# Encoder layer with attention, retention and a mixture of experts: retention moved beside the input projection, a block at a time, and the overflow tables moved two jobs later

## The chip, the cores and the metric

The program runs on one core of one Trainium2 chip. The metric is the device time of one execution, in microseconds (us), lower being better. TensorE (PE) does the matmuls, VectorE (DVE), ScalarE (ACT) and GpSimd (POOL) the elementwise work, and SyncE (SP) issues most of the transfers between HBM and the on-chip memories SBUF and PSUM. Each engine runs its own queue of instructions strictly in order.

## The reference, cut to what matters

```python
xn = rmsnorm(x, attn_norm_g); proj = xn @ w_in          # 2048 x 1024 by 1024 x 3072
q_da, k_da, v_da, q_r, k_r, v_r, g_r = split(proj)
o_da = diff_attention(...)        # 4 heads, two softmax maps each, ALiBi, block-causal
# retention, 4 heads, chunkwise recurrent:
s = einsum(q, k * 64**-0.5) * decay ** (i - j)          # lower triangle
intra = s @ v
state = state * decay ** CHUNK + (k * k_decay).T @ v
o_r = silu(g) * head_rmsnorm(intra + (q * q_decay) @ state)
h = x + concat(o_da, o_r) @ w_out
xn = rmsnorm(h, ffn_norm_g)
out = rmsnorm(h + moe(xn), final_norm_g)                # 32 experts, 2 of them for each token
```

Only retention is changed in its formula: if a key is divided by its decay when it is written, then scores need no more than a mask, and what is left over is one factor for each query row, which a norm over the head removes, apart from its epsilon.

## The kernel before

All sizes are float32; large matmuls are made of three float32r products of a high and a low part (`mm3`: hi by hi, hi by lo, lo by hi), so each operand is first split by ACT (the high part, a copy) and DVE (the low part, a subtraction). The time falls into these parts.

- **The input projection** (`Proj.run`) goes through a list of units. A unit is one 128x512 piece of the projected columns for one group of 512 tokens or one block of 128 rows: 24 matmuls into the PSUM tile `pa`. Kind 2 is the values of attention, 1 and 0 its keys and queries, 3 the queries and keys of retention, 4 and 5 its values and gates. The list has three stages (token groups 0 and 1, then 2, then 3). In each stage of the kernel before, all kinds 2, 1 and 0 come first and 3, 4 and 5 last. The weights of a unit are loaded as `wr` and split into `whi` and `wlo`. Results go to scratch in HBM (`VS`, `KS`, `QS`, `RT`, `VR`, `GR`).
- **Attention** (`att_head`) runs for each stage and head over blocks of 128 queries: score matmuls into `pS`, each followed on DVE by one instruction that adds the distance bias and takes the maximum (`p<-pS,dist`, L352), the exponential on ACT, on DVE the difference of the two maps (`p<-p,c,p`, L366), then transposes into `pT`, a split of them on ACT and DVE (`ah` and `al`), and matmuls with the values into `pO`.
- **Retention** (`retention`) takes two blocks of 128 tokens at a time: POOL multiplies values and queries by decays (`vd`, `qd`) and finishes the outputs (`O`).
- **The output projection** (`OutProj`) loads and splits `w_out` (`woh`, `wol`), and then makes each block of 128 rows of `h` by matmuls into `pF`, its norm and its router logits.
- **The experts** (`experts`) run as 32 jobs. A job gathers its rows (`xg`), transposes them on DVE (`xT`), splits weights (`mh`, `ml`) and multiplies. Between the jobs' matmuls stand steps of `units` and `completion`, which make the tables for experts that overflow and the order in which rows are finished (tiles `u_...` and `c_...`); the first such step stands in job `SIDE`.

`merge` writes two parts into one program by their planned weights: attention beside the projection until a share `FA` of attention is written, then beside retention (`FR`), and the rest beside the output projection. `OutProj.steps` takes block b only when `k.ready` is over b, and block 11 only when all attention is written. A scheduler then fixes each engine's order.

Of the kernel before, what the change touches and what calls it, by code (L numbers as in the profile page):

```python
# [24 lines left out]
EPS = 1e-6  # L25
# [59 lines left out]
class Proj:  # L85


    def __init__(self, k, ctx):
# [15 lines left out]
        self.ready = set()  # L104
        self.nload = self.nsplit = 0
        units = []
        for s, gs in enumerate(STAGES):
            bs = [4 * g + i for g in gs for i in range(4)]
            units += [(2, b) for b in bs]
# [84 lines left out]
    def colT(self, u, c, ct, g):  # L194
# [8 lines left out]
        if c == 3:  # L203
            st = self.stg.tile([128, 512], F32, name="st", tag="st")
            nc.scalar.activation(st, ps, AF.Copy)
            nc.sync.dma_start(k.RT[ct][:, ts], st)
            return
# [9 lines left out]
    def rows(self, u, c, b):  # L217
# [14 lines left out]
        else:  # L232
            st = self.stg.tile([128, 512], F32, name="st", tag="st")
            nc.scalar.activation(st, ps, AF.Copy)
            nc.sync.dma_start((k.VR if c == 4 else k.GR)[bs, :], st)

    def run(self):
# [10 lines left out]
        for u, x in enumerate(self.units):  # L248
# [3 lines left out]
            elif n0 - 4 <= u < n0:  # L252
                nb = u - n0 + 12
            elif n0 + 4 <= u < n0 + 12 and u % 2 == 0:
                nb = (u - n0 - 4) // 2 + 12
# [9 lines left out]
            else:  # L265
                yield from self.rows(u, *x)


def attention(k, pj):

    with ExitStack() as ctx:
        att_psum(k, ctx)
        for s in range(len(STAGES)):
# [4 lines left out]
            with ExitStack() as c1:  # L278
                att_pools(k, c1, s)
                for h in range(4):  # L280
                    while (s, h) not in pj.ready:
                        yield 0
                    yield from att_head(k, s, h)
    k.att_done, k.ready = True, NB
    yield 0.1

# [9 lines left out]
def att_head(k, s, h):  # L296
# [26 lines left out]
    U = k.bu.tile([128, nq, 128], F32, name="U")  # L323
# [3 lines left out]
    def scores(i):  # L327

        if i % 2 == 0:
            q = k.bq.tile([128, 2, 2, 256], F32R, name="qs")  # L330
            for m in range(2):
                for d in range(2):
                    nc.sync.dma_start(q[d * 64:(d + 1) * 64, m].bitcast(F32),
                                      k.QS[h][:, m * 64:(m + 1) * 64, i * 128:(i + 2) * 128].rearrange("i d t -> d i t"))
            qs[0] = q
        o = i % 2 * 128
# [5 lines left out]
        for m in range(2):  # L342
# [4 lines left out]
            for n, (a0, a1) in enumerate(ch):  # L347
                acc = k.pS.tile([128, 512], F32, name="pS")
                x = acc[:, :a1 - a0]
                nc.tensor.matmul(x, qs[0][:, m, 0, o:o + 128], ks[m][:, a0:a1], start=True, stop=False)  # L350
                nc.tensor.matmul(x, qs[0][:, m, 1, o:o + 128], ks[m][:, a0:a1], start=False, stop=True)  # L351
# [17 lines left out]
    def values(j):  # L369
# [34 lines left out]
        oT = k.bo.tile([128, 256], F32, name="oT")  # L404
# [5 lines left out]
        jj = 2 * (j - 2 * g0)  # L410
        for ii in range(2):
            nc.scalar.activation(U[:, jj + ii], pt[:, 0, ii * 128:(ii + 1) * 128], AF.Square, accum_out=ss[:, jj + ii:jj + ii + 1])
        nc.scalar.activation(U[:, jj:jj + 2].rearrange("p a b -> p (a b)"), pt[:, 0], AF.Copy)
        yield 0.2

    def finish(b0, b1):
# [8 lines left out]
        u = U[:, b0:b1]  # L425
        nc.gpsimd.tensor_mul(u, u, r[:, :, None].to_broadcast([128, n, 128]))  # L426
        nc.gpsimd.tensor_mul(u, u, k.subg[:, None, :].to_broadcast([128, n, 128]))
# [8 lines left out]
    step = 2 if (s, h) == (len(STAGES) - 1, 3) else nq  # L436
    done = 0
    for j in range(n0, n1):
        yield from scores(2 * j)
        if j > n0:  # L440
            load_rest()
            yield from values(j - 1)
            if 2 * (j - n0) % step == 0:
                finish(done, done + step)
                done += step
                if step == 2:
# [6 lines left out]
def retention(k):  # L453
    nc, tc = k.nc, k.tc
    V, G = nc.vector, nc.gpsimd
    state, qz = [], {}
    for pr in range(2):
        s_ = k.br.tile([128, 128], F32, name=f"state{pr}", bufs=1)
        V.memset(s_, 0.0)
        state.append(s_)  # L460
        for n in range(2):
            z = k.br.tile([128, 2, 256], F32, name=f"qz{pr}{n}", bufs=1)
            V.memset(z[0:64, 1], 0.0)
            V.memset(z[64:128, 0], 0.0)
            qz[pr, n] = z
    def prepare(n):
        X = K()
        X.rows = ts = slice(n * 256, n * 256 + 256)
        X.kt = k.br.tile([128, 2, 256], F32, name="kt")
        for i in range(2):  # L470
            nc.sync.dma_start(X.kt[:, i], k.RT[2 + i][:, ts])
        X.q = [qz[pr, n % 2] for pr in range(2)]
        for pr in range(2):
            for s in range(2):
                nc.sync.dma_start(X.q[pr][s * 64:(s + 1) * 64, s], k.RT[pr][s * 64:(s + 1) * 64, ts])
        X.vr = k.br.tile([128, 2, 512], F32, name="vr")
        gr = k.br.tile([128, 2, 512], F32, name="gr")
        nc.sync.dma_start(X.vr, k.VR[ts, :].rearrange("(b p) n -> p b n", p=128))
        nc.sync.dma_start(gr, k.GR[ts, :].rearrange("(b p) n -> p b n", p=128))
        X.vd = k.br.tile([128, 2, 4, 128], F32, name="vd")  # L480
        G.tensor_mul(X.vd, X.vr.rearrange("p b (h e) -> p b h e", h=4),
                     k.vdec[:, None, :, None].to_broadcast([128, 2, 4, 128]))
        X.qd = []
        for pr in range(2):
            qd = k.br.tile([128, 2, 2, 128], F32, name=f"qd{pr}")
            G.tensor_mul(qd, X.q[pr].rearrange("p s (b t) -> p s b t", b=2),
# [1440 lines left out]
```

## Time and profile before

| | us |
|---|---|
| median of 3 runs | 2099.15 |
| lowest and highest of them | 2093.79, 2099.17 |
| the profiled execution's own time | 2083.01 |
| its span, first to last instruction | 2081.2 |

The rows below come from the profiled execution, and all times in them are counted from the start of its span. Its own time is 1.8 us more than the span, and 16.1 us under the median of the runs.

### The profile page before, as it was taken

How to read it: one execution, taken by the hardware profiler on the slowest of the kernel's cores; microseconds unless marked ns; L12 is line 12 of the kernel's file. 1: busy time of each engine (PE TensorE's matmuls, PEld its weight loads, DVE VectorE, ACT ScalarE, POOL GpSimd, SP SyncE). 2: the span in 40 equal slices, each digit the busy share in tenths (PEclk: the TensorE clock that was granted, in tenths of full speed). 3: DMA queues.
4: the chain of work that ended last, by engine and by line, in shares of the span. 5: the costliest groups of instructions: out<-in, count | busy, mean ns of one | idle time of the engine just before them, and what ended most of it. 6: DMA issues, size and time to landing. Idle time of an engine off the chain costs nothing.

```text
span 2081.2 us, 30110 instructions
## 1 busy us (share of the span) xinstructions
PE 1944.9 (93%) x9811; PEld 1543.9 (74%) x9811; DVE 1553.2 (75%) x3462; ACT 1122.7 (54%) x1915; POOL 673.7 (32%) x362
## 2 busy tenths in 40 slices
PE   7999999999999987789999996799999999999994
PEld 5788888878888875578887775577777677777673
DVE  7345446855565578987877767999988899998884
ACT  4244445634444454555454314676776787776663
POOL 0000000010000037421111105566867667875433
PEclk9999999999999998899999997799999999999997
DMA  6655344573675456463453455799999999998994
GB/s 201 193 153 171 117 135 144 178 242 129 195 213 167 137 160 215 128 203 132 156 183 111 138 223 182 254 304 296 338 343 320 319 339 349 353 344 302 338 316 117
DMA packets 241810, 459.61 MB, mean 221 GB/s; under 512 B 27376, under 2 KB 130160, under 8 KB 240624
## 3 DMA queue, kind: packets, MB, share of 16 engines
q1 hardware_dynamic: 224384, 401.53, 56.9%
q0 software_dynamic: 16976, 55.06, 9.8%
q8 instruction: 78, 1.28, 0.3%
q10 hardware_dynamic: 288, 1.05, 0.1%
q14 instruction: 84, 0.69, 0.1%
HBM read 365.81 MB, written 91.75 MB: 220 GB/s over the span
## 4 chain that ended last, share of the span: by engine, by line
PE 72%; DVE 9%; DMA 7%; issue 5%; SPq 2%; POOL 2%; ACT 2%; ACTq 0%; DVEq 0%; POOLq 0%
PE pa L63 7%; PE pa L62 7%; PE pa L64 7%; PE acc L63 7%; PE acc L62 7%; PE acc L64 7%; PE acc L72 4%; PE acc L74 3%; PE pS L350 3%; PE pS L351 3%; PE pT L382 2%; PE pF L62 2%; PE pF L64 2%; PE pF L63 2%; DMA wr<-in_w_in_dram 2%
## 5 line engine op out<-in xcount | busy, mean ns | idle before, releaser
L1485 DVE TENSOR_TENSOR ml<-mr,mh 128x1024 fp32r<-128x1024 f32 x376 | 446.5, 1214 | 38.6 <-ACT mh L1484 32.4
L1484 ACT ACTIVATE mh<-mr 128x1024 fp32r<-128x1024 f32 x376 | 385.5, 1055 | 124.0 <-PE acc L74 66.3
L1515 POOL DMA_INDIRECT xg<-XN,TA x120 | 270.0, 2250 | 64.3 <-issue 30.5
L352 DVE CUSTOM_DVE_ANT_0 p<-pS,dist 128x512 f32<-128x512 f32 (+1 forms) x320 | 188.0, 605 | 126.3 <-PE pS L351 118.5
L426 POOL TENSOR_TENSOR U<-U,r 128x512 f32<-128x512 f32 (+2 forms) x13 | 16.5, 1270 | 725.9 <-DVE r L40 623.9
L359 ACT ACTIVATE p<-p,nm 128x128 f32<-128x128 f32 (+15 forms) x128 | 153.9, 1203 | 111.8 <-DVE nm L358 111.5
L63 PE MATMUL acc<-ml,xhi 128*128 128x512 f32 x512 | 205.9, 403 | 5.0 <-DVE ml L1485 5.0
L64 PE MATMUL acc<-mh,xlo 128*128 128x512 f32 x512 | 206.2, 403 | 1.3 <-DVE xlo L1557 1.3
L62 PE MATMUL acc<-mh,xhi 128*128 128x512 f32 x512 | 204.0, 401 | 0.0
L54 ACT ACTIVATE ah<-pT 128x512 fp32r<-128x512 f32 (+2 forms) x176 | 85.4, 498 | 141.1 <-PE pT L382 99.6
L62 PE MATMUL pa<-xh,whi 128*128 128x512 f32 x384 | 152.9, 398 | 2.0 <-DVE nlam L633 2.0
L62 PE MATMUL pa<-whi,xh 128*128 128x512 f32 x384 | 151.8, 398 | 2.9 <-ACT whi L161 2.1
L63 PE MATMUL pa<-wlo,xh 128*128 128x512 f32 x384 | 153.1, 399 | 1.5 <-DVE nm L358 1.2
L64 PE MATMUL pa<-whi,xl 128*128 128x512 f32 x384 | 153.9, 401 | 0.0
L63 PE MATMUL pa<-xl,whi 128*128 128x512 f32 x384 | 151.8, 395 | 0.0
L64 PE MATMUL pa<-xh,wlo 128*128 128x512 f32 x384 | 151.6, 395 | 0.0
L350 PE MATMUL pS<-kst,qs 128*128 128x512 f32 (+1 forms) x320 | 123.5, 398 | 21.6 <-DVE cm L352 8.9
L162 DVE TENSOR_TENSOR wlo<-wr,whi 128x1024 fp32r<-128x1024 f32 x72 | 89.9, 1250 | 67.0 <-ACT whi L161 64.4
L55 DVE TENSOR_TENSOR al<-pT,ah 128x512 fp32r<-128x512 f32 (+2 forms) x176 | 97.5, 564 | 44.9 <-ACT ah L54 44.4
L62 PEld LDWEIGHTS acc<-mh,xhi 128*128 128x128 f32 x512 | 97.3, 190 | 31.8 <-ACT xhi L54 0.2
L161 ACT ACTIVATE whi<-wr 128x1024 fp32r<-128x1024 f32 x72 | 76.1, 1059 | 81.2 <-DMA wr<-in_w_in_dram 39.9
L63 PEld LDWEIGHTS acc<-ml,xhi 128*128 128x128 f32 x512 | 97.6, 191 | 28.9 <-DVE ml L1485 5.4
(536 smaller groups left out, 4912.5 us busy)
## 6 DMA issues: line engine op xcount, KB each, us to landing
mr<-in_expert_w_gate_dram SPq DMA_DIRECT2D x128, 512.0 KB
mr<-in_expert_w_up_dram SPq DMA_DIRECT2D x128, 512.0 KB
mr<-in_expert_w_down_dram SPq DMA_DIRECT2D x128, 512.0 KB
wr<-in_w_in_dram SPq DMA_DIRECT2D x72, 512.0 KB
vst<-VS SPq DMA_DIRECT2D x72, 256.0 KB
qs<-QS SPq DMA_DIRECT2D x128, 128.0 KB
st<-in_x_dram SPq DMA_DIRECT2D x16, 512.0 KB
VS<-st SPq DMA_DIRECT2D x32, 256.0 KB
```

What stands on the lines that cost most here:

```text
L54: nc.scalar.activation(hi, ps, AF.Copy)
L55: return nc.vector.tensor_sub(lo, ps, hi.bitcast(F32))
L62: nc.tensor.matmul(out, s_hi, m_hi, start=start, stop=False)
L63: nc.tensor.matmul(out, s_hi, m_lo, start=False, stop=False)
L64: nc.tensor.matmul(out, s_lo, m_hi, start=False, stop=stop)
L162: nc.vector.tensor_sub(lo, r, hi.bitcast(F32))
L350: nc.tensor.matmul(x, qs[0][:, m, 0, o:o + 128], ks[m][:, a0:a1], start=True, stop=False)
L352: nc.vector.tensor_tensor_reduce(p[:, a0:a1], x, tab[:, c0 + a0:c0 + a1], SLOPES[h], -3.0e38, OP.add, OP.max, accum_out=cm[:, n:n + 1])
L359: nc.scalar.activation(p[:, :nk], p[:, :nk], AF.Exp, bias=nm, accum_out=s0 if m == 0 else s1)
L1484: self.hi_at = nc.scalar.activation(hi, r, AF.Copy)
L1485: self.lo_at = nc.vector.tensor_sub(lo, r, hi.bitcast(F32))
L1515: nc.gpsimd.indirect_dma_start(out=xg[:, g * 256:(g + 1) * 256], out_offset=None, in_=v, in_offset=bass.IndirectOffsetOnAxis(ap=ix[:, g], ...
```

## The change

- Projection: in stages 0 and 2, kinds 3, 5 and 4 (in this order) follow the first head instead of the last. Keys of retention are multiplied by the inverse decay `kdec` as they leave PSUM (on DVE), and gates are written as silu(g) times two (tanh on ACT, one DVE instruction).
- `mixer` takes the place of `attention`: in stages 0 and 2 it writes retention (blocks 0 to 7, then 8 to 15) in turns with the attention of that stage, by `strands`, in proportion to planned weights. Stage 1 has attention alone. `mixers` goes on with `mixer` alone, after the projection, until the last block of retention is written (`k.kept_all`), and then merges what is left with the output projection.
- `retention` takes one block at a time; it uses the PSUM tiles `pT` of attention and `pt` of the projection. POOL's multiplications (`vd`, `qd`, `O`, `U`, half of `wol`) are gone: their work is left out by the new formula or done on DVE.
- The factor `subg` of attention's outputs goes into `w_out`. Queries of attention are loaded a block at a time with two buffers instead of two blocks at a time with one.
- Experts: `SIDE` is 3 instead of 1, and the rows of job 2 are transposed one step later (q 3 instead of q 2 of job 1).

```diff
 class Proj:
+            heads = []
             for h in range(4):
-                units += [(1, h, g) for g in gs] + [(0, h, g, s) if g == gs[-1] else (0, h, g) for g in gs]
-            units += [(3, h, g) for h in range(4) for g in gs]
-            units += [(c, b) for c in (4, 5) for b in bs]
+                heads.append([(1, h, g) for g in gs] + [(0, h, g, s) if g == gs[-1] else (0, h, g) for g in gs])
+            rest = [(3, h, g) for h in range(4) for g in gs] + [(c, b) for c in (5, 4) for b in bs]
+            if s != 1:
+                heads.insert(1, rest)
+            else:
+                heads.append(rest)
+            units += [(2, b) for b in bs] + sum(heads, [])
...
+                a = heads()
+                if s != 1:
+                    b0, b1 = RB[s]
+                    with k.tc.tile_pool(name=f"br{s}", bufs=2, reuse_waits="tile") as k.br:
+                        yield from until(lambda: k.kept == b1, (a, att_weight(s)), (retention(k, pj, b0, b1), (b1 - b0) * R_W))
+                    k.kept_all = b1 == NB
+                yield from a
+            if s < 2:
+                k.ready = 512 * (STAGES[s][-1] + 1) // 128
...
+RB = {0: (0, 8), 2: (8, 16)}
+R_W = 3.8
...
-        nc.gpsimd.tensor_mul(u, u, r[:, :, None].to_broadcast([128, n, 128]))
-        nc.gpsimd.tensor_mul(u, u, k.subg[:, None, :].to_broadcast([128, n, 128]))
+        u = U[0] if end else U[0][:, b0:b1]
+        nc.vector.tensor_mul(u, u, r[:, :, None].to_broadcast([128, n, 128]))
...
+            po = pj.pst.tile([128, 4, 128], F32, name="pt").rearrange("p a b -> p (a b)")
             for s in range(2):
+                h = 2 * pr + s
+                v = X[pr][1][:, s * 128:(s + 1) * 128]
                 if b:
+                    nc.tensor.matmul(po[:, s * 128:(s + 1) * 128], qz[pr][:, s], k.state[pr], start=True, stop=False)
+                nc.tensor.matmul(po[:, s * 128:(s + 1) * 128], A[:, s], v, start=not b, stop=True)
+                if b < NB - 1:
+                    nc.tensor.matmul(po[s * 64:(s + 1) * 64, 256:384], kd[:, s], v, start=True, stop=True)
...
+        for h in range(4):
+            V.scalar_tensor_tensor(th[:, h], O[:, h], r[:, h:h + 1], th[:, h], op0=OP.mult, op1=OP.mult)
...
 def mixers(k, outer):
-    na = att_weight()
+    na = sum(att_weight(s) for s in range(3))
+    nr = NB * R_W
...
-        merge(tc, pj.run(), 96 * 5.1 + 16 * 1.9, a, na * FA, 76)
+        merge(tc, pj.run(), 96 * 5.1 + 16 * 1.9, a, na * FA + nr, 76)
+        while not k.kept_all:
+            with tc.high_priority(PRI):
+                next(a)
     router_setup(k)
-        ret_consts(k)
-        merge(tc, retention(k), 58, a, na * FR)
...
-        merge(tc, op.blocks(at), OB, a, na * (1 - FA - FR))
+        merge(tc, op.blocks(at), OB, a, na * (1 - FA))
...
-SIDE = 1
+SIDE = 3
...
-                if q == 2 and n + 1 < 32:
-                    if n < 31:
-                        loads(n - 2)
-                    if n:
+                if q == 2 and n < 31:
+                    loads(n - 2)
+                if q == (3 if n == 1 else 2) and n + 1 < 32:
+                    if n == 1:
+                        with tc.issue_after(m.lo_at.ins):
+                            m.rows(jobs[2])
+                    elif n:
                         m.rows(jobs[n + 1])
```

How the queues stand, at three places. The first is PE at the end of the input projection in the kernel before: the last matmuls of the projection (`pa`), then attention, among which the first of retention (`pF<-qz,kt`) follows some 30 rows on.

```order
L62 MATMUL pa<-whi,xh_4227 128x512
L63 MATMUL pa<-wlo,xh_4227 128x512
L64 MATMUL pa<-whi,xl_4228 128x512
L62 MATMUL pO<-ah,vst 128x256
L350 MATMUL pS<-kst,qs 128x512
L351 MATMUL pS<-kst,qs 128x512
L350 MATMUL pS<-kst,qs 128x512
L351 MATMUL pS<-kst,qs 128x512
L63 MATMUL pO<-al,vst 128x256
```

In the changed kernel the same place reads as follows, and 1,208 PE instructions of attention and of retention's blocks 8 to 15 stand between the last `pa` and the first matmul of the output projection, where 594 (346 of attention, 248 of retention) stood before.

```order
L64 MATMUL pa<-xh_4949,wlo 128x512
L62 MATMUL pa<-xh_4949,whi 128x512
L63 MATMUL pa<-xl_4950,whi 128x512
L64 MATMUL pa<-xh_4949,wlo 128x512
L417 MATMUL pS<-kst,qs 128x512
L418 MATMUL pS<-kst,qs 128x512
L417 MATMUL pS<-kst,qs 128x512
L418 MATMUL pS<-kst,qs 128x512
L476 MATMUL pT<-ident,oT 128x128 x2
L449 MATMUL pT<-ident,p_5733 128x128
```

The second place is PE at the first matmuls of the output projection (`pF<-woh,mh`) in the changed kernel, which stand among the score matmuls of the last head.

```order
L417 MATMUL pS<-kst,qs 128x512
L418 MATMUL pS<-kst,qs 128x512
L792 MATMUL pF<-ident,mx 128x128 x8
L417 MATMUL pS<-kst,qs 128x384
L418 MATMUL pS<-kst,qs 128x384
L62 MATMUL pF<-woh,mh 128x512
L63 MATMUL pF<-wol,mh 128x512
```

Behind it 166 PE instructions of attention are left, where 614 were left before. The third place is PE in job 1 of the experts, before: the tables' matmul `pt<-u_tri,u_w` stands ahead of the transposes `pt<-ident,sg` of job 0's hidden rows.

```order
L62 MATMUL acc<-mh,xhi 128x512
L63 MATMUL acc<-ml,xhi 128x512
L64 MATMUL acc<-mh,xlo 128x512
L1282 MATMUL pt<-u_tri,u_w 128x32
L1594 MATMUL pt<-ident,sg 128x128 x4
L1287 MATMUL pt<-ident,u_w 128x32
L62 MATMUL acc<-mh,hhi 128x512
```

In the changed kernel those transposes stand earlier, among the matmuls of job 1, and the tables' matmul comes 193 rows later.

```order
L62 MATMUL acc<-mh,xhi 128x512
L63 MATMUL acc<-ml,xhi 128x512
L64 MATMUL acc<-mh,xlo 128x512
L62 MATMUL acc<-mh,xhi 128x512
L1651 MATMUL pt<-ident,sg 128x128 x4
L62 MATMUL acc<-mh,xhi 128x512
L63 MATMUL acc<-ml,xhi 128x512
```

## Rows read from the trace of the kernel before

**Rows 1.** Page, part 1: busy time of each engine, its share, instructions.

```profile
PE 1944.9 (93%) x9811; PEld 1543.9 (74%) x9811; DVE 1553.2 (75%) x3462; ACT 1122.7 (54%) x1915; POOL 673.7 (32%) x362
```

**Rows 2.** Tiles `wlo`, `wol`, `woh`, `pa`: min/median/max ns, first and last start in us.

```profile
L162 DVE TENSOR_TENSOR wlo<-wr,whi x72: 1215/1224/3108, 10.7 to 709.5; 128x1024 fp32r<-128x1024 f32 x72
...
L64 PE MATMUL pa<-whi,xl x384: 387/393/775, 14.7 to 736.8; 128*128 128x512 f32 x192
...
L713 DVE TENSOR_TENSOR wol<-wor,woh x4: 1207/1390/2111, 902.4 to 908.9; 128x1024 fp32r<-128x1024 f32 x4
...
L62 PE MATMUL pF<-woh,mh x256: 387/393/632, 912.1 to 1247.2; 128*128 128x512 f32 x128
```

**Rows 3.** Busy time by stage: length, PE, PEld, DVE, ACT, POOL, clock, DMA.

```profile
0.00:709.50 709.50, 686.75 (x3443) 574.42 (x3444) 408.34 (x1147) 317.25 (x632) 27.74 (x55) 1.00 0.55 170
709.50:737.20 27.70, 27.70 (x145) 23.41 (x144) 14.16 (x46) 11.17 (x21) 2.33 (x2) 1.00 0.39 114
737.20:902.40 165.20, 125.87 (x789) 100.59 (x788) 140.36 (x364) 86.91 (x286) 88.05 (x49) 0.88 0.54 175
912.10:1248.10 336.00, 326.10 (x2027) 269.93 (x2025) 253.82 (x866) 139.25 (x263) 41.25 (x34) 0.99 0.48 161
1248.10:1325.00 76.90, 46.58 (x181) 35.52 (x182) 61.16 (x158) 35.44 (x43) 50.35 (x28) 0.69 0.55 188
```

**Rows 4.** PE in order of time, 693.9 to 694.5 us: start, duration, instruction.

```profile
693.95 0.40 PE L351 MATMUL pS<-kst,qs 128*128 128x512 f32 x1
694.19 0.28 PE L63 MATMUL pO<-al,vst 128*128 128x256 f32 x1
694.31 0.28 PE L64 MATMUL pO<-ah,vst 128*128 128x256 f32 x1
```

**Rows 5.** Groups on DVE, shapes apart: busy us, mean ns | idle before them.

```profile
L352 DVE CUSTOM_DVE_ANT_0 p<-pS,dist 128x512 f32<-128x512 f32 x224 | 150.8, 685 | 78.9 <-PE pS L351 71.3 <-PE pT L382 6.1
L55 DVE TENSOR_TENSOR al<-pT,ah 128x512 fp32r<-128x512 f32 x112 | 75.3, 685 | 39.8 <-ACT ah L54 39.5
...
L502 DVE TENSOR_TENSOR A<-pF,rdec 128x256 f32<-128x256 f32 x32 | 13.3, 415 | 3.2 <-PE pF L500 3.1
L491 DVE SCALAR_TENSOR_TENSOR th<-th,gr 128x1024 f32<-128x1024 f32 x8 | 11.4, 1430 | 2.3 <-DMA qs<-QS 2.3
L530 DVE SCALAR_TENSOR_TENSOR state<-state,sdec,pF 128x128 f32<-128x128 f32 x30 | 10.2, 339 | 7.1 <-PE pF L528 6.8
L352 DVE CUSTOM_DVE_ANT_0 p<-pS,dist 128x128 f32<-128x128 f32 x32 | 9.2, 287 | 24.5 <-PE pS L351 24.5
L40 DVE SCALAR_TENSOR_TENSOR r<-t,r 128x4 f32<-128x4 f32 x21 | 3.3, 159 | 0.5
```

**Rows 6.** The same, 790 to 900 us: two groups.

```profile
L352 DVE CUSTOM_DVE_ANT_0 p<-pS,dist 128x512 f32<-128x512 f32 x32 | 21.5, 680 | 2.6 <-PE pS L351 2.6
...
L366 DVE SCALAR_TENSOR_TENSOR p<-p,c,p 128x1664 f32<-128x1664 f32 x2 | 6.8, 3418 | 0.0
```

**Rows 7.** The same, 930 to 1160 us: two groups.

```profile
L366 DVE SCALAR_TENSOR_TENSOR p<-p,c,p 128x2048 f32<-128x2048 f32 x3 | 7.0, 2346 | 0.1
...
L366 DVE SCALAR_TENSOR_TENSOR p<-p,c,p 128x1664 f32<-128x1664 f32 x2 | 3.9, 1952 | 0.1
```

**Rows 8.** Busy time in three shorter stretches, columns as in the stages.

```profile
770.00:800.00 30.00, 22.76 (x139) 18.14 (x138) 19.42 (x57) 11.46 (x56) 20.98 (x12) 0.82 0.90 284
810.00:900.00 90.00, 65.39 (x417) 52.09 (x416) 84.70 (x210) 51.53 (x144) 41.42 (x20) 0.91 0.41 138
1170.00:1247.00 77.00, 73.66 (x410) 56.79 (x407) 59.35 (x309) 16.54 (x39) 3.79 (x4) 0.98 0.56 213
```

**Rows 9.** PE's waits, 1248 to 1325 us: waited for, us, times, longest.

```profile
PE pt L1282 <- DVE u_w L1291: 10.8, 1, 10.8
PE acc L63 <- DVE ml L1485: 5.0, 1, 5.0
```

**Rows 10.** DVE's waits, 1281 to 1325 us.

```profile
DVE xT L1554 <- DMA xg<-XN,TA: 7.1, 1, 7.1
```

More of the change, by code (lines that the diff above doesn't have):

```diff
@@ L266, in run, with strands, mixer @@
                 yield from self.rows(u, *x)
-def attention(k, pj):
+                if x[0] == 4:
+                    self.rt = x[1] + 1
+def strands(*gs):
+    st = [[g, w, w, 0.0, False] for g, w in gs]
+    while st:
+        for x in sorted(st, key=lambda x: x[3] / x[2]):
+            w = next(x[0], None)
+            if w is None:
+                st.remove(x)
+                break
+            if w == 0:
+                x[4] = True
+                continue
+            if x[4]:
+                x[4] = False
+                for y in st:
+                    y[2], y[3] = max(y[1], 0.1), 0.0
+            x[1] -= w
+            x[3] += w
+            yield w
+            break
+        else:
+            yield 0
+def mixer(k, pj):
     with ExitStack() as ctx:
         att_psum(k, ctx)
+        ret_consts(k, ctx)
         for s in range(len(STAGES)):
@@ L279, in attention, with heads, until @@
                 att_pools(k, c1, s)
[L280 to L283, printed above, removed]
+                def heads():
+                    for h in range(4):
+                        while (s, h) not in pj.ready:
+                            yield 0
+                        yield from att_head(k, s, h)
+                a = heads()
[7 more added lines that the diff above has]
+                k.ready = 512 * (STAGES[s][-1] + 1) // 128
     k.att_done, k.ready = True, NB
     yield 0.1
+def until(done, *gs):
+    for w in strands(*gs):
+        yield w
+        if done():
+            return
+RB = {0: (0, 8), 2: (8, 16)}
+R_W = 3.8
 S_W = 0.108
@@ L327, in scores @@
     def scores(i):
[L329 to L336, printed above, removed]
+        for ii in (i, i + 1):
+            if ii not in qs and ii < 4 * g1:
+                q = qs[ii] = k.bq.tile([128, 2, 2, 128], F32R, name="qs")
+                for m in range(2):
+                    for d in range(2):
+                        nc.sync.dma_start(q[d * 64:(d + 1) * 64, m].bitcast(F32),
+                                          k.QS[h][:, m * 64:(m + 1) * 64, ii * 128:(ii + 1) * 128].rearrange("i d t -> d i t"))
+        q = qs.pop(i)
         nk = (i + 1) * 128
@@ L435, in load_rest @@
             pass
-    step = 2 if (s, h) == (len(STAGES) - 1, 3) else nq
+    step = 2 if end else nq
     done = 0
@@ L445, in att_head @@
                 done += step
-                if step == 2:
+                if end and h == 3:
                     k.ready = 4 * g0 + done
@@ new lines, in inner @@
+    def inner(kt, pr):
+        pa = k.pT.tile([128, 2, 256], F32, name="pT").rearrange("p a b -> p (a b)")
+        nc.tensor.matmul(pa[:, :256], kt, qz[pr], start=True, stop=True)
+        nc.tensor.transpose(pa[:, 256:384], kt, k.ident)
+        A = k.br.tile([128, 2, 128], F32, name="A")
+        V.tensor_mul(A, pa[:, :256].rearrange("p (s c) -> p s c", s=2), k.msk[:, None, :].to_broadcast([128, 2, 128]))
+        kd = k.br.tile([128, 2, 64], F32, name="kd")
+        for s in range(2):
+            nc.scalar.activation(kd[:, s], pa[:, 256 + 64 * s:320 + 64 * s], AF.Copy, scale=math.exp(128 * LGAM[2 * pr + s]))
+        return A, kd
@@ L526, in retention @@
             if b < NB - 1:
[L527 to L530 removed]
+                V.scalar_tensor_tensor(k.state[pr], k.state[pr], k.sdec[:, pr:pr + 1], po[:, 256:384], op0=OP.mult, op1=OP.add)
@@ L665 @@
+    for x in k.state:
+        nc.vector.memset(x, 0.0)
 class OutProj:
@@ L936 @@
 FA = 0.7
-FR = 0.12
 AT = 10
```

249 lines of the change are left out of this document (110 added, 139 removed).

## The prediction

> **What bounds the kernel now.** I read the page first. PE is busy 93% of the span and DVE 75% [rows 1], so the question is where PE is not busy, and what it waits for there. The ends of four tiles cut the span [rows 2]: the last split of projection weights starts on DVE at 709.5 us, the last matmul of the projection starts at 736.8 (with its 0.39 us it ends at 737.2), DVE starts on the weights of the output projection at 902.4, and that projection's matmuls go from 912.1 to 1248.1. Busy times by stage [rows 3] then show three kinds of stretch. Beside the projection PE is full (686.75 of 709.5) and DVE idles for four tenths (408.34). After it, where attention and retention run without a large matmul beside them, DVE is busy for 140.36 of 165.2 us and PE for 125.87: **here DVE is the bound**. From 810 to 900 it has 84.70 of 90 [rows 8]; the loss lies at the change of stage and in the start of retention, 770 to 800, with 19.42 of 30. Beside the output projection PE is full again (326.10 of 336). So attention costs little where PE has large matmuls beside it, and what DVE needs where it has none. The change must be priced by how much DVE work it puts into the middle stretch.
>
> **What moves.** Retention's own stretch goes: blocks 0 to 7 stand beside the projection. But retention needs its columns, so while they are projected in stage 0 only the first head of attention can be written, and `mixers` goes on without a partner until retention's last block is written. `strands` hands out turns in proportion, so that block comes when stage 2's attention is almost done too. The queues show it: between the last split `wlo` and the first `wol` DVE had 58 score instructions, 28 splits `al` and 8 differences of maps; it will have 172, 90 and 23. Attention's PE instructions beside the projection fall from 1,152 to 861, and beside the output projection from 614 to 166.
>
> **The projection.** On PE 291 instructions of attention leave it. A score matmul takes 0.24 us from start to start and a value matmul 0.12 [rows 4]; I take a transpose at 0.12 too, and 0.14 for narrower scores. 64 wide and 24 narrow scores, 89 transposes and 114 value matmuls make 15 + 3 + 11 + 14 = 43 us. 125 instructions of retention come in. The trace has no spacing for them that is not mixed with waits: 0.12 us is the lower bound (15 us), and the upper is what is left of PE's 125.87 us [rows 3] after 346 attention instructions at 0.14, 77 us for 248, 0.31 each (39 us). They are float32 and closer to the upper one: 31. So 12 us fewer: the projection ends at 725. DVE's new work there (half of retention, the keys' decay, the gates) is some 50 us, less than the attention that leaves, and DVE has 300 us idle beside a full PE; if that cover failed it would cost at most those 50. The two extra weight loads and the query loads in twice as many pieces lie on SP and behind PE in the same way.
>
> **The middle stretch.** DVE's work in it, priced by its groups [rows 5]: of 172 scores 136 are 512 wide at 0.685 us, the others between 0.287 and that, say 0.42: 93 + 15. Splits: 66 wide at 0.685 and 24 narrow at 0.35: 45 + 8. Differences of maps: 37,632 columns at 1.16 ns, from 1952 ns for 1664 and 2346 for 2048 [rows 7]: 44. Retention: 16 masks at 0.415 as for `A`, 14 states and 32 scalings at 0.339: 7 + 16. Some 298 tiny ones (roots, maxima, reciprocals) at 0.159: 47. Nine multiplications of `U` that POOL did, 5 evacuations of the projection and a few constants: 14. Together 289, say **290 us, against 154.5 now** (14.16 + 140.36 [rows 3]). As a check, the stretch of before priced alike, with 8 `th` at 1.43 us [rows 5], comes to 144, and what POOL adds to it (below) to 8 more: 152 for 154.5.
>
> Some 14 us of the 290 lie ahead of the projection's end as now (the last `wlo` stands five evacuations ahead of it; 14.16 today). 276 are left. At full use of DVE they last 276 us, at 94% (810 to 900 [rows 8]) 294, at 85% (737.2 to 902.4 [rows 3]) 325. The stretch holds one change of stage, and one run of 62 PE instructions of retention with no attention among them, as the bad 770 to 800 had; but it holds far more attention. I take 90%: 307. Then 10 us from the first `wol` to the first matmul (902.4 to 912.1 [rows 2]); DVE now makes all eight splits, which could make that 15. So 317 us where 174.9 were.
>
> **The output projection.** Beside it 448 PE instructions of attention are gone: 116 wide and 28 narrow scores, 124 transposes, 180 value matmuls: 27 + 4 + 15 + 22 = 68 us. 326 - 68 = 258 us busy; at the share of 1170 to 1247, where it already runs nearly alone (73.66 of 77 [rows 8]), 270 instead of 336.
>
> **The start of the experts.** PE waited 10.8 us for a tables' step on DVE that stood ahead of the next transposes, and 5.0 for a weight split [rows 9], which stood behind a transpose that itself waited 7.1 for its gather [rows 10]. Both orders change. What is gained lies between nothing (DVE is busy 61.16 of 76.9 there [rows 3], and PE then waits for its splits) and both waits, 16; I take 8. The tables come later into jobs where PE is full, and are not needed before job 11.
>
> **Sum.** 725 + 317 + 270 = 1312 for the end of the output projection, 64 more than 1248; less 8: **56 us more**. The profiled execution took 2083 (span 2081.2), so it would take 2139. The median of the runs is 16 us over that execution, and I keep that distance: 2099 + 56 = **2155**. With full use of DVE and both waits gained it is 725 + 286 + 270 - 16, +17, thus 2116; with 85%, 15 us for the splits and no gain at the start, 725 + 340 + 270, +87, thus 2186.
>
> **Rivals.**
> *A, DVE's instructions get shorter, since POOL is silent: faster.* POOL was busy for 88.05 of 165.2 us [rows 3], and a 1664-wide difference took 3418 ns there [rows 6] against 1952 later [rows 7]. For no change the stretch may last 725 + x + 270 - 8 = 1248, x = 261: 251 us of DVE at full use, 9% under 276. At 15% less it is 235 + 10, thus 16 us faster: 2083. Against it: the score instruction took 680 ns in that stretch [rows 6] and 685 over the whole kernel [rows 5], most of it with POOL idle, and my prices are already those without POOL. The Trainium skill (SBUF — State Buffer, "Who interferes with whom") says that a DVE instruction with two SBUF inputs contends with a GpSimd instruction that reads SBUF, and that one with at most one such input, outside the two-port modes, does not. By it scores and splits, which read PSUM, gain nothing, the stretch stays at 276 and this rival falls; the two groups agree. Chance 0.06.
>
> *B, PE becomes the bound: slower still.* PE's work in the stretch, 1,208 instructions, is some 190 us by the spacings above, 60% of 317. Where PE was busy for 65.39 of 90 us its granted clock was 0.91 [rows 8], and 0.69 at 46.58 of 76.9 [rows 3]. At 0.69 it needs 275 us and stays hidden; at the lower of its two levels, 1.2 GHz, throughout, it needs 380: 725 + 390 + 270 - 8, +129, thus 2228. The Trainium skill (TensorE: Matmul & The Clock Gate, "HAM oscillation — how this bites in real kernels") tells of kernels whose pauses put PE back to the low level again and again. That speaks against the change; no row of this trace has a long stretch in which it stays there. Chance 0.05.
>
> *C, nothing to be seen.* The stretch costs what the other parts give back, x = 261 within 6 us: DVE would have to run at 97% or more with 9% less work than counted, or the order beside the projection would have to save another 50 us, where PE has only 23 idle. Chance 0.04.
>
> **Chances.** Forecast 0.85, of which 0.05 lie outside 2112 to 2190; A 0.06; B 0.05; C 0.04. Measurement tells no change from one of 0.3%, 6 us. Faster 0.06, same 0.04, slower 0.90. The range 2112 to 2190 is that of the bounds above with 4 us on either side for the runs' own spread.
>
> **What would show it.** Right: the last `pa` near 725; DVE over 85% busy for some 300 us after it, with PE near 60%; `pF<-woh` from about 1040 to 1312, with PE over 95%; no wait of 10 us for `u_w` in job 1; POOL idle in the middle. Wrong: the stretch under 260 us, its scores under 0.6 us each; or DVE under 80% there, with PE's waits on chains of retention (`state`, `qz`) or on key loads; or the projection over 740, because retention's waits hold up PE's queue.

## The result: 2206.85 us, 5.3% slower, outside the forecast range

| | before | changed |
|---|---|---|
| median of 4 runs, us | 2096.47 | 2206.85 |
| lowest and highest, us | 2092.73, 2099.17 | 2201.85, 2213.68 |
| profiled execution's span, us | 2081.2 | 2204.7 |

The ratio is 1.0534 (95% interval 1.0502 to 1.0566). The forecast was slower, but 2155 and at most 2190: in the traces the change costs 123.5 us where 56 were forecast. The page of the changed kernel, busy times of the engines (beside [rows 1]):

```profile
PE 2025.3 (92%) x9811; PEld 1579.4 (72%) x9811; DVE 1571.7 (71%) x3690; ACT 1122.6 (51%) x1929; POOL 553.9 (25%) x293
```

PE has as many instructions as before and is busy 80 us longer. The tiles that cut the span [rows 2], in the changed kernel (columns: min/median/max ns, first and last start):

```profile
L169 DVE TENSOR_TENSOR wlo<-wr,whi x74: 1212/1226/1228, 11.2 to 705.4; 128x1024 fp32r<-128x1024 f32 x74
...
L64 PE MATMUL pa<-xh,wlo x384: 387/389/628, 69.9 to 734.9; 128*128 128x512 f32 x192
...
L62 PE MATMUL pF<-woh,mh x256: 387/396/632, 1098.7 to 1380.0; 128*128 128x512 f32 x128
```

The projection ends at 735.3 (737.2 before), the output projection starts at 1098.7 (912.1) and ends at 1380.9 (1248.1). The same stretches as in [rows 3], columns as there:

```profile
0.00:705.40 705.40, 683.25 (x3373) 565.01 (x3374) 398.67 (x1178) 301.07 (x674) 5.19 (x47) 0.99 0.56 170
...
735.30:1098.40 363.10, 273.68 (x1323) 207.40 (x1322) 259.32 (x823) 165.83 (x372) 1.84 (x1) 0.82 0.43 127
...
1098.40:1381.00 282.60, 268.37 (x1578) 213.88 (x1576) 171.95 (x625) 85.59 (x169) 27.96 (x24) 0.97 0.39 143
1381.00:1460.00 79.00, 62.28 (x273) 48.73 (x273) 71.48 (x155) 51.75 (x62) 50.20 (x27) 0.85 0.68 237
```

In the middle DVE is busy for 259.32 of 363.10 us (71%), PE for 273.68 (75%) at a granted clock of 0.82, and POOL is silent. No engine is full. Two pieces of it show the spread:

```profile
940.00:970.00 30.00, 20.89 (x74) 14.26 (x75) 13.54 (x59) 6.63 (x35) 0.00 (x0) 0.64 0.26 81
...
1030.00:1060.00 30.00, 24.86 (x139) 19.30 (x138) 25.75 (x80) 18.09 (x40) 0.00 (x0) 0.94 0.47 140
```

At 940 stands the run of retention without attention: DVE at 45%. At 1030 it is attention with a little of retention: 86%. The waits from 735.3 to 1081.6 us (waited for: us, times, longest), first DVE's, then PE's:

```profile
DVE al L55 <- ACT ah L54: 25.9, 23, 3.4
DVE p L419 <- PE pS L418: 18.1, 36, 2.6
DVE A L550 <- PE pT L548: 17.8, 13, 4.1
DVE state L583 <- PE pt L581: 16.3, 11, 3.5
```

```profile
PE pO L63 <- DVE al L55: 9.7, 11, 2.4
PE pS L417 <- DVE cm L419: 9.1, 25, 1.2
PE pT L449 <- DVE p L433: 8.3, 7, 1.7
PE pt L578 <- ACT O L587: 6.0, 5, 1.5
PE pT L547 <- DMA qz<-RT: 5.3, 3, 2.4
```

In the kernel before, the same four waits of DVE read as follows, 737.2 to 902.4 us:

```profile
DVE state L530 <- PE pF L528: 6.8, 3, 4.2
DVE A L502 <- PE pF L500: 3.1, 3, 2.2
DVE p L352 <- PE pS L351: 2.6, 5, 1.3
DVE al L55 <- ACT ah L54: 2.5, 3, 1.9
```

DVE waits for PE and ACT, PE for DVE and ACT: a chain, in which each waits for the next in turn. The four rows of DVE come to 78 of 346 us, where they were 15 of 165; 44 us are attention's (the first two rows), 34 retention's. Transfers are part of it: of PE's 77.5 us of waits 25.6 end on one, that is the row of `qz` and others on attention's keys and queries. The chain of work that ended last (followed back from step to step to what released each), from 735 to 1100 us:

```profile
by line: PE pS L417 8.2%; DVE p L419 7.7%; DVE p L433 7.3%; PE pT L449 6.2%; PE pS L418 5.8%; DVE al L55 5.1%; issue 4.7%; DMA qs<-QS 4.4%; PE pO L63 3.4%; DMA qz<-RT 3.4%; PE pt L578 3.2%; ACT p L426 3.0%; PE pt L581 2.9%; DMA kst<-KS 2.9%
```

It has many small parts, none over 8.2%. Of what the row lists, PE has 30%, DVE 20% and transfers 11%.

### The profile page after: what moved, and what is told of

Same layout as the page of the kernel before. It is cut to its first block, busy times and chain, and to the rows that moved or that the text cites. A ratio compares the mean times of both kernels' runs of the same rounds, so it can differ in the third digit from the quotient of the medians.

```text
span 2204.7 us, 30653 instructions
## 1 busy us (share of the span) xinstructions
PE 2025.3 (92%) x9811; PEld 1579.4 (72%) x9811; DVE 1571.7 (71%) x3690; ACT 1122.6 (51%) x1929; POOL 553.9 (25%) x293
## 4 chain that ended last, share of the span: by engine, by line
PE 71%; DVE 9%; DMA 8%; issue 5%; POOL 3%; ACT 2%; SPq 1%; ACTq 0%; DVEq 0%; POOLq 0%
PE pa L62 7%; PE pa L64 7%; PE pa L63 7%; PE acc L63 6%; PE acc L64 6%; PE acc L62 6%; PE acc L72 3%; PE acc L74 3%; PE pF L64 3%; PE pF L62 3%; PE pS L417 3%; PE pF L63 3%; PE pT L449 2%; PE pS L418 2%; POOL xg L1572 2%
## 5 line engine op out<-in xcount | busy, mean ns | idle before, releaser
L1572 POOL DMA_INDIRECT xg<-XN,TA x120 | 274.8, 2290 | 69.8 <-issue 30.8
L419 DVE CUSTOM_DVE_ANT_0 p<-pS,dist 128x512 f32<-128x512 f32 (+2 forms) x320 | 187.6, 607 | 93.8 <-PE pS L418 79.4
L417 PE MATMUL pS<-kst,qs 128*128 128x512 f32 (+1 forms) x320 | 137.1, 436 | 30.8 <-DVE cm L419 12.1
L914 POOL TENSOR_TENSOR xc<-xT 128x512 bf16<-128x512 f32 x24 | 28.0, 1165 | 469.0 <-ACT xT L911 453.8
L449 PE MATMUL pT<-ident,p 128*128 128x128 f32 x544 | 110.6, 297 | 20.6 <-DVE p L433 8.5
```

What stands on the lines that cost most here:

```text
L417: nc.tensor.matmul(x, q[:, m, 0], ks[m][:, a0:a1], start=True, stop=False)
L419: nc.vector.tensor_tensor_reduce(p[:, a0:a1], x, tab[:, c0 + a0:c0 + a1], SLOPES[h], -3.0e38, OP.add, OP.max, accum_out=cm[:, n:n + 1])
L449: nc.tensor.transpose(pt[:, t, ii * 128:(ii + 1) * 128], ab[ii][:, (t0 + t) * 128:(t0 + t + 1) * 128], k.ident)
L1572: nc.gpsimd.indirect_dma_start(out=xg[:, g * 256:(g + 1) * 256], out_offset=None, in_=v, in_offset=bass.IndirectOffsetOnAxis(ap=ix[:, g], ...
```

## The experiments

All start from the changed kernel, except E4; E9 leaves out the work of retention's blocks 8 to 15. Stretches come from the first and last matmuls of `pa` and `pF` in each trace; "att" counts attention's PE instructions in the queue beside the projection, in the middle, and beside the output projection (E5's with the repeats); "rest" is from the end of the output projection to the end of the span. Where an expectation speaks of the first set, its runs are E1 to E4 in this order. The sets are E1 to E4, E5 to E8, E9 to E11 and E12 to E14, each on another chip; the kernel before, run again with each, had medians of 2081 to 2088 us. So the ratios compare better from set to set than the medians do.

| kernel | att | projection ends | middle | output projection | rest | median, ratio to before [interval] |
|---|---|---|---|---|---|---|
| before | 1152/346/614 | 737.2 | 174.9 | 335.9 | 833.1 | |
| changed | 861/1085/166 | 735.3 | 363.4 | 282.2 | 823.8 | 2207, 1.0534 [1.0502, 1.0566] |
| E1 | 1189/757/166 | 844.1 | 273.4 | 283.7 | 825.5 | 2227, 1.0673 [1.0625, 1.0722] |
| E2 | 861/713/538 | 733.2 | 263.5 | 331.0 | 825.4 | 2155, 1.0334 [1.0298, 1.0371] |
| E3 | 1189/385/538 | 846.8 | 177.9 | 327.7 | 822.6 | 2180, 1.0449 [1.0397, 1.0502] |
| E4 | as before | 738.1 | 179.4 | 336.1 | 826.7 | 2083, 0.9952 [0.9916, 0.9987] |
| E5 | 861/1196/183 | 734.1 | 366.7 | 284.3 | 833.1 | 2218, 1.0610 [1.0583, 1.0637] |
| E6 | 861/1087/164 | 733.0 | 360.8 | 277.9 | 833.2 | 2205, 1.0544 [1.0498, 1.0589] |
| E7 | 946/1000/166 | 773.6 | 333.2 | 283.8 | 839.7 | 2230, 1.0647 [1.0592, 1.0701] |
| E8 | 1215/405/492 | 888.5 | 170.0 | 313.8 | 827.4 | 2201, 1.0535 [1.0500, 1.0571] |
| E9 | 837/83/1192 | 737.3 | 28.2 | 489.7 | 822.4 | 2077, 0.9960 [0.9929, 0.9990] |
| E10 | 1033/541/538 | 775.4 | 225.4 | 326.6 | 813.1 | 2152, 1.0342 [1.0304, 1.0381] |
| E11 | 861/713/538 | 733.9 | 262.0 | 328.8 | 829.9 | 2158, 1.0368 [1.0338, 1.0398] |
| E12 | 1215/415/482 | 894.5 | 177.0 | 312.4 | 818.1 | 2204, 1.0584 [1.0552, 1.0616] |
| E13 | 953/592/567 | 746.4 | 229.7 | 330.0 | 820.8 | 2125, 1.0242 [1.0162, 1.0321] |
| E14 | 907/717/488 | 754.6 | 258.0 | 314.1 | 830.5 | 2160, 1.0368 [1.0311, 1.0425] |

### Where attention stands: E1, E2, E3

E1, columns of retention last in stage 0:

```diff
-            if s != 1:
+            if s == 2:
                 heads.insert(1, rest)
```

> The changed kernel, but in stage 0 the retention's columns (kinds 3, 5, 4) are projected last again, as before; in stage 2 they stay second. By the planned order 1,189 attention instructions on PE then stand beside the projection (861 in the changed kernel), 880 of attention and retention between the last `pa` and the first `pF<-woh` (1,208), 166 behind it (166). Theory D (displaced attention): the middle stretch costs 0.30 us for each of its PE instructions (363 us for 1,208 in the changed kernel, 175 for 594 in the kernel before), and an attention instruction beside large matmuls 0.12. So the projection ends at 735 + 39 = 774, the stretch takes 264, the output projection 282 as now: 61 us less than the changed kernel, 2146. Theory C (retention's own chains and loads): DVE's work in the stretch runs at 90% and some 72 us of waits are retention's, whatever attention is there; then the stretch takes 295 and the kernel 2177.

E2, retention's blocks first in the turns of stage 2:

```diff
-(a, att_weight(s)), (retention(k, pj, b0, b1), (b1 - b0) * R_W)
+(a, att_weight(s) / (6 if s == 2 else 1)), (retention(k, pj, b0, b1), (b1 - b0) * R_W)
```

> The changed kernel, but in stage 2 the weight of attention in the turns is divided by 6, so that retention's blocks 8 to 15 get their turns first and the output projection may begin while attention is left over. Columns are projected as in the changed kernel. Planned order on PE: 861 attention instructions beside the projection (861), 836 in the middle stretch (1,208), 538 beside the output projection (166). Theory D: projection 735, stretch 836 x 0.30 = 251, output projection 282 + 372 x 0.12 = 327, together 68 us less: 2139. Theory C: stretch 286, 33 us less: 2174.

E3, both:

> Both edits of the two runs above together: retention's columns last in stage 0, and its blocks first in the turns of stage 2. Planned order on PE: 1,189 beside the projection, 508 in the middle stretch, 538 beside the output projection; thus nearly the kernel before, with half of retention out of the stretch. Theory D: projection 774, stretch 508 x 0.30 = 152, output projection 327, 128 us less than the changed kernel: 2079, thus under the kernel before (2097). Theory C: stretch 219, 61 us less: 2146, still slower than before.

The middle stretch came out nearer to theory D, though 10 to 26 us over it: 273.4 (264), 263.5 (251) and 177.9 (152), against 295, 286 and 219 by theory C; the output projection came out as D has it: 283.7, 331.0, 327.7 (282, 327, 327). By the traces E2 gives 52 us back by moving 372 attention instructions from the middle to where large matmuls run; its 2155 lies midway between D's 2139 and C's 2174. A line through changed, E1, E2, E3 and E10 (below) fits to 5 us: 79 us plus 0.261 for each attention instruction. The 79, which do not go with attention, are what theory C had and D had not. But E1 and E3 ended their projection 70 us later than forecast, and E1 was slower than the changed kernel. Both theories missed that; E13 finds it.

### The start of the experts: E4, E11

E4, the kernel before with `SIDE = 3` and the rows of job 2 a step later:

> The kernel before with the last part of the change alone: SIDE 3, and the rows of job 2 one step later. Theory D: the start of the experts gains on its own what the traces show between the end of the output projection and the end of the span (833 us before, 824 in the changed kernel): 9 us less, 2088. Rival: the 9 us come from what the other parts leave at the end of the output projection (less attention there), and this part alone gains nothing: 2097.

E11, E2 with this part as before:

> The kernel of the second run of the first set (retention's blocks first in the turns of stage 2, 2155), with SIDE 1 and the rows of job 2 at their old step, thus the expert part as before. Theory W (the two waits at the start of the experts are what this part of the change removes, whatever stands ahead): 5 to 9 us slower, 2160 to 2164, with the 10.8 us wait for `u_w` back in job 1. Rival (the part is worth nothing here): 2155 within 3 us.

E4 is faster than before by 0.5% (0.1 to 0.8%, thus 3 to 18 us, 5 by the medians; theory D asked for 9), the only version here that beats both kernels and leaves nothing out. In E11 the wait of [rows 9] is back, and in E2 it is not there (PE's waits of E11, 1320 to 1420 us):

```profile
PE pt L1339 <- DVE u_w L1348: 11.7, 1, 11.7
```

Its median is 3 us over E2's, but the intervals overlap. So that the wait goes is shown, and that the part gains in the kernel before; its size behind the other parts is not measured.

### What bounds the middle: E5, E6

E5, one more matmul ahead of each score in stage 2:

```diff
+                if s == 2:
+                    nc.tensor.matmul(x, q[:, m, 0], ks[m][:, a0:a1], start=True, stop=True)
                 nc.tensor.matmul(x, q[:, m, 0], ks[m][:, a0:a1], start=True, stop=False)
```

> The changed kernel, but in stage 2 of attention the first score matmul of each chunk is issued once more ahead of itself (128 more PE instructions, 109 of them in the middle stretch; the sums stay as they were, since the repeat is overwritten). Theory P (PE at its lower clock is the bound of the stretch, clock 0.82 there): each repeat lengthens it by the spacing of a score matmul, 0.24 us at the higher of the two levels and about twice that at the lower: 26 to 52 us slower, 2233 to 2259. Theory L (attention alone goes from engine to engine and waits; PE has 79 us without work there): the repeats go into PE's idle time, 2207 within 10 us.

E6, queries two blocks at a time:

```diff
-        for ii in (i, i + 1):
+        for ii in (i, i + 1) if i % 2 == 0 else ():
```

> The changed kernel, but the queries of attention are loaded two blocks at a time again, as before the change (two tiles side by side, issued together at every second block). Theory Q (the loads of single blocks arrive late): PE's waits on `qs` in the middle stretch, 4.7 + 4.5 + 1.6 us, go: some 11 us less, 2196. Theory L: the pieces are hidden; 2207 within 6 us.

Theory L in both, though E5's 2218 is 1 us more than it allowed. E5's middle is 3.3 us longer for 111 more PE instructions, where theory P asked for 26 to 52. Of the 13.5 us between its trace and the changed kernel's, 9.3 lie in "rest", where its code is that of the changed kernel, and E6, of the same set, has the same rest without repeats. From 735 to 1090 us, first the changed kernel, then E5:

```profile
735.00:1090.00 355.00, 271.85 (x1315) 205.55 (x1313) 254.12 (x812) 161.66 (x368) 1.84 (x1) 0.83 0.42 124
```

```profile
735.00:1090.00 355.00, 279.44 (x1413) 217.68 (x1410) 251.41 (x798) 159.07 (x362) 1.84 (x1) 0.87 0.41 121
```

PE took 98 more instructions in the same time, and the granted clock rose from 0.83 to 0.87. So more work on PE does not lengthen the stretch, and PE is not its bound as theory P has it. But the matmuls that were there before also ran shorter in E5 (a transpose of `p` 308 ns instead of 319, the second matmul of a 512-wide score 427 instead of 448), so part of the repeats was paid for by the clock. What the stretch would take if PE ran at the higher level throughout, no run shows. In E6 PE waits on `qs` no more (10.8 us in the changed kernel), and the stretch is 2.6 us shorter: the query loads of single blocks are hidden all but this. Key loads (`kst`, 5.2 us of PE's waits) were not tried.

### Retention's chain: E7, E8, E12, E14

E7 and E8, two buffers for `qz` with the next block's loads ahead of this block's outputs, alone and on E3 (`st` with three buffers instead of four makes room):

> The changed kernel, but retention's queries `qz` have two buffers, and the next block's loads are issued ahead of this block's outputs; three buffers instead of four for the projection's results `st` make room. The planned order changes a little too: 946 attention instructions beside the projection (861), 1,000 in the middle (1,085), 166 behind. The four kernels measured so far give the stretch as 76 us plus 0.265 us for each attention instruction in it. Theory S (the single buffer makes retention a chain of load, scores, outputs, load): the 76 us shrink by a load of some 2 us for each of the 16 pairs, the stretch takes 309, the projection 8 more: 2161. Theory L: the 76 us stay, the stretch takes 341: 2193.

> The kernel with retention's columns last in stage 0 and its blocks first in stage 2, with two buffers for `qz` as in the run above. Planned order on PE: 1,215 attention instructions beside the projection, 405 in the middle, 492 beside the output projection. In the kernel with one buffer retention's blocks 0 to 7 stood in a row from 394 to 490 us, each pair waiting for its `qz` load (2.0 to 3.2 us), and the projection ended at 847 instead of 774. Theory S: the loads leave that row, 16 x 2 to 3 us, so the projection ends near 810, the stretch takes 151 and the output projection 322: 2110. Theory L2 (the row is held by the steps between PE, DVE and ACT, not by the loads): projection 847, stretch 183, output projection 322: 2182.

E12 and E14, all loads ahead, on E3 and on E2:

```diff
+        vr = k.br.tile([128, 256], F32, name="vr", bufs=4)
...
+        for pr in range(2):
+            if b + 1 < min(b1, pj.rt):
+                nxt[pr] = load(b + 1, pr)
+        nc.sync.dma_start(th, k.GR[bs, :].rearrange("p (h e) -> p h e", h=4))
```

> As the kernel with two buffers for `qz`, retention's columns last in stage 0 and its blocks first in stage 2 (2201), but now nothing of a block's loads waits for the block ahead: four buffers for `vr`, and the load of the gates `th`, which waits for the last block's store, stands behind the next block's loads in SP's queue. In the run before, the second buffer of `qz` hardly showed: its loads were still issued late, behind `vr` and `th`. Theory S (loads hold retention's row in stage 0): a pair's period there falls from some 6 us to under 4.5, the row gets 25 us or more shorter, and the kernel takes 2175 or less. Theory L2 (the row goes from engine to engine: scores, mask, outputs, three instructions of ACT on the one `pt` tile): period 5.5 to 6, 2200 as before.

> Retention's blocks first in the turns of stage 2 (2155), with all of retention's loads ahead (two buffers of `qz`, four of `vr`, the gates' load behind them; three buffers of `st` in the projection). Planned order: 907 attention instructions beside the projection (861), 717 in the middle (713), 488 behind (538). Theory S: retention's 70 us of the stretch, 123 instructions (what is left of the 76 when the start is taken off), shrink by 2 us for each of 16 pairs: stretch 234, 2124. Theory L2: stretch 266, 2156.

The loads are not what mainly holds retention. Against the line, which itself fits to 5 us, the middle lost 7 us in E7, 8 in E14, 15 in E8 and 10 in E12, not 32, and retention's row in stage 0 kept its 5 to 7 us a pair in E12 (score matmuls of pairs start at 421.1, 428.0, 433.9, 439.7, 445.5, 450.9). None got faster: the projection ended 21 us (E14 against E2) to 48 us (E12 against E3) later, of which 3 to 10 go with more attention beside it at 0.12 each. The remainder may be the three buffers for `st`, which came with it; it was not tried alone. PE's waits in E12's row, 390 to 500 us, now name the chain as often as the load:

```profile
PE pT L551 <- DMA qz<-RT: 6.1, 3, 2.8
PE pt L586 <- ACT O L595: 6.0, 3, 4.3
PE pT L551 <- ACT O L595: 3.2, 2, 1.7
PE pT L551 <- DVE t L39: 2.5, 1, 2.5
```

### Retention taken out, or moved: E9, E10

> The changed kernel with the work of retention's blocks 8 to 15 left out (their rows of the result are filled with the gates; blocks 0 to 7 and all of attention stay). Attention's order then follows from the same turns, but nothing of retention is left behind the projection, and the planned order has 83 attention instructions between the last `pa` and the first `pF<-woh` (1,085) and 1,192 behind it (166). Theory G (what holds the output projection back is retention's last block, and attention is dear only because it stands where no large matmul is): projection 733, stretch 83 x 0.265 and a start of some 25 us, 47; output projection 282 + 1,026 x 0.12 = 405; then 824 as now: 2011. Theory E (attention costs its 0.265 us wherever DVE must do it): output projection 282 + 1,026 x 0.265 = 554, in all 2160. Retention's own share would then be small either way.

> Retention's blocks first in the turns of stage 2, as in the second run of the first set, and in stage 0 retention's columns behind the second head (first in the changed kernel, fourth in the kernel whose projection stalled at 390 to 490 us). Planned order on PE: 1,033 attention instructions beside the projection, 541 in the middle, 538 behind. Theory D with cover (retention's row costs the projection nothing where other units of the projection stand between its steps): projection 735 + 172 x 0.12 = 756, stretch 76 + 541 x 0.265 = 219, output projection 329, then 824: 2130. Rival (any later place makes projection wait for the row, by half of the 70 us or more): 2165 or more, no better than 2155.

In E9 the output projection starts at once, so it was retention's last block that held it back. Its stretches (columns as in [rows 3]):

```profile
737.30:765.50 28.20, 18.04 (x92) 14.19 (x92) 24.60 (x54) 18.85 (x29) 0.00 (x0) 0.76 0.81 261
765.50:1255.10 489.60, 442.95 (x2599) 358.19 (x2597) 369.35 (x1243) 213.14 (x403) 31.85 (x25) 0.95 0.43 143
```

Neither theory holds: 2077 lies between 2011 and 2160. The output projection took 489.7, between theory G's 405 and E's 554: (489.7 - 282.2) / 1,026 = 0.20 us for each more attention instruction, where 372 more in E2 cost 0.13. That so much attention finds too few large matmuls is the likely reading; no run varies it further. The middle of 28.2, less 83 at 0.261, is 6.5; by this estimate some 72 of the line's 79 us are retention's, 0.59 for each of its 123 instructions. E10's middle (225.4, forecast 219) is on the line, but its projection ended 19 us later than forecast, so it gained nothing over E2.

### The tile `pt`: E13

```diff
-            po = pj.pst.tile([128, 4, 128], F32, name="pt").rearrange("p a b -> p (a b)")
+            po = k.pT.tile([128, 2, 256], F32, name="pT").rearrange("p a b -> p (a b)")
```

> Retention's columns last in stage 0 and its blocks first in stage 2 (2180), but retention's outputs use attention's tiles `pT` (two buffers) instead of the projection's single `pt`. Planned order: 953 attention instructions beside the projection (1,189), 592 in the middle (385), 567 behind (538). Theory T (the single tile `pt` makes each pair wait until ACT has taken the pair ahead): a pair's period in the row of stage 0 falls from 5.9 us to under 4.5, the projection ends near 790 (819 without an effect: 847 less 236 x 0.12). Theory L2: period as before, projection 819, stretch 76 + 592 x 0.265 = 233, output projection 332, in all 2210.

The projection ended at 746.4, 100 us earlier than E3's; by estimate 28 of them go with the 236 attention instructions fewer beside it (0.12 each), 72 do not. Theory T asked for 790. The same 30 us in E3 and in E13:

```profile
440.00:470.00 30.00, 23.36 (x76) 16.15 (x75) 12.25 (x51) 7.18 (x33) 0.00 (x0) 0.53 0.28 90
```

```profile
440.00:470.00 30.00, 29.57 (x147) 23.06 (x146) 17.54 (x51) 12.12 (x37) 0.00 (x0) 1.00 0.87 228
```

In E3 retention's row stands there alone; in E13 the projection's matmuls stand between its steps, PE is full, and a pair takes 6 to 11 us (425.5, 436.3, 445.3, 451.2) without costing anything. The projection needs `pt` for the transposes of the next rows of x (`pt<-ident,st`), and in E1 and E3 these stood behind retention's outputs in the one buffer: from 385 us on the next came at 462 in E3, at 389 in E13. So theory T named the right tile, but not its effect: the pairs did not get faster. The middle (229.7, the line gives 233.5) did not change either. At 2125 this is the fastest version with the whole of the new retention, still 1.6 to 3.2% slower than before. The tile was not tried in the changed kernel's own order.

## Why the prediction was wrong, point by point

- **What moves: right.** Attention's share of each stretch came out as stated, and E1, E2 and E3 show that the time of the middle follows it.
- **Projection, 725 forecast, 735.3 measured.** Attention that left was priced at 43 us; if that is right, then with 1.9 gained retention's 125 instructions cost 41, 0.33 each, a little over the upper bound of 0.31. No run separates the two.
- **The middle, 317 forecast, 363.4 measured: the step that failed.** "I take 90%" for DVE's use: DVE was taken as the bound, and here no engine is. The work itself was over-priced: up to the first `wol` at 1081.6 us DVE was busy for 246 us where 276 were forecast. The use was 71%, below the lowest rate that I allowed (85%), and 70% in E2; so this part took 346 us instead of 307. (The other 7 us lie behind it: 17 from the first `wol` to the first matmul, where 10 were forecast, 8 of them on the chain for a load of `mx`.) The sign of being wrong that the prediction named, DVE under 80% with PE's waits on `qz` and key loads, is what came. The 90% was chosen between [rows 3] and [rows 8], pieces with two streams in which retention took two blocks at a time. By the line, if attention cost the same there, before's retention cost 0.31 us for each of its 248 instructions ((174.9 - 6.5 - 346 x 0.261) / 248), the new one 0.59; about 4.9 against 9.1 us a block. The one row that showed the rate of a stretch with retention without cover, 770 to 800 with 19.42 of 30, was named and then put down as an exception. In the changed kernel the run of 62 lasts 44 us (937.3 to 981 us), with DVE busy for 44%. But outside this run, where attention and the rest of retention stand together, DVE is busy for 75% only, so the run is not the whole of it. Attention carries the rest: 1,085 at 0.261 are 283 us, more than all of DVE's 259.
- **The output projection, 270 forecast, 282.2 measured.** PE is busy 95% as forecast; its work is 268 us, not 258. 448 attention instructions fewer gave back 54 us, 0.12 each, not 68.
- **The start of the experts, 8 forecast.** The traces show 9.3, but "rest" is 823.8 to 839.7 in kernels with the same code there (changed, E5, E6, E7). E4 is the evidence, with 3 to 18 us; that the 8 fits is in part luck.
- **The reference point.** I added the forecast to the median, 16 us over the profiled execution. The changed kernel's profiled execution is its median, so the medians differ by 110 and the traces by 123.5. By the traces the sum is 67 us short (10 + 46 + 12, less 1), by the median 52: the choice of the median as the starting point hid the difference, by luck.
- **Rival A falls.** POOL is silent, and the score instruction takes 687 ns (680 with POOL at work [rows 6]). DVE's groups from 735.3 to 1081.6 us:

```profile
L419 DVE CUSTOM_DVE_ANT_0 p<-pS,dist 128x512 f32<-128x512 f32 x130 | 86.8, 687 | 18.9 <-PE pS L418 15.8 <-PE pT L449 2.2
...
L433 DVE SCALAR_TENSOR_TENSOR p<-p,c,p 128x1664 f32<-128x1664 f32 x4 | 7.8, 1946 | 0.1
```

The difference of maps, with two SBUF inputs, does get shorter there (1946 ns, 3418 in [rows 6]). The Trainium skill (SBUF — State Buffer, "Who interferes with whom") has a DVE instruction with two SBUF inputs contend with a GpSimd instruction that reads SBUF, and one with at most one such input, outside the two-port modes, not; both groups agree.
- **Rival B was near, and is not the cause as it was put.** PE is busy for 273.7 us of the stretch instead of some 190, at a granted clock of 0.82 between its levels of 1.2 and 2.4 GHz (0.64 at 940 to 970, where PE had waited between short matmuls). E5 shows that PE's work fits in, so PE is not full; that its lower clock makes the steps of the chain longer is not ruled out, and PE's steps are the largest part of the chain that ended last.
- **What stays open.** The loads explain 7 to 15 us of the middle at most and the tile `pt` none of it, and more work on PE does not lengthen it. That it is the way from PE to DVE to ACT and back, with the next block's scores issued only behind this block's outputs, is what remains, and the waits fit it; no run shows it by itself, nor how much of it is PE's lower clock. Issuing the scores ahead, as the kernel before does, was not tried.

## What to carry to other kernels

Price work by what stands beside it: attention cost 0.13 us an instruction where 372 were put beside large matmuls, 0.20 where 1,026 were, and 0.26 without cover. So the count of attention instructions left without cover told the middle to 5 us wherever retention's loads were left as they were, and the sum of DVE's durations did not. Take the rate of a stretch from one with the same streams in the same form: here DVE reached 71%, where the old form of retention beside attention had 85 to 94%. And a single buffer shared by two parts (`pt`) can stop the part that ought to be the cover.

## Not expected of the hardware

The expert part after the output projection varies more than I allowed: 813.1 to 839.7 us over the kernels with `SIDE = 3`, with one trace of each and on several chips, so that chip, execution and the part ahead are not separated here. E4's ten runs, one kernel on one chip, go from 2058.9 to 2085.6 us. Gains under 1% there need repeated runs, not one trace. And 98 more matmuls in the same 355 us came with a higher granted clock (0.83 to 0.87): PE's busy time grew by 8 us only, 0.08 each.
